# A one-layer hybrid decoder trunk: values times weights by key block, four recurrent heads in one group of score pieces, gates ahead of the attentions, a new order of the first loads

## The chip, the cores and the metric

The kernel runs on one core of one Trainium2 chip. The metric is the device time of one execution in microseconds (us). Of the engines, PE is the matrix engine (PEld its weight loads), DVE the vector engine, ACT the scalar engine, POOL the general one, SP the engine that here only issues DMAs. "PSUM" are the accumulator banks into which PE writes.

## The reference, cut to what matters

```python
# x: 512 tokens x 1024; mem: 256 tokens x 1024; all float32
h = rmsnorm(x, norm_mix)
# one input projection: c_q 384, c_kv 256, k_rope 64, hg q, f, i, g 4 x 512, mem q 512
o_a = mla_group(...)      # 4 heads, 192-wide q and k, causal softmax, values 128 wide
o_b = hgrn2_group(...)    # 4 recurrent heads:
    q = silu(q_raw) * 128 ** -0.5
    f = lb + (1 - lb) * sigmoid(f_raw);  k = 1 - f
    # out_t = sum over s <= t of (q_t . (prod of f over s+1..t) . k_s) v_s
    o = rmsnorm(o, out_gain) * silu(g_raw)
o_c = mem_group(...)      # 4 heads, softmax over the 256 memory tokens
x = x + rmsnorm-ed groups @ w_out
x = x + swiglu(rmsnorm(x), w_gate, w_up, w_down)   # hidden width 2816
```

## The kernel before

**Arithmetic.** Each float32 product of large matrices is done as three matmuls of rounded parts (`mm3`): an operand is split (`split`) into a rounded high part, copied by ACT (`xh`, `wh`, `pth`), and the rest, subtracted by DVE (`xl`, `wl`, `ptl`). Weights come in pieces of 512 columns, so that each piece costs one ACT copy and one DVE subtraction of 128x512.

**Order.** `body` does not issue instructions. A recorder notes each operation with its engine, inputs and a priority (its place in the program, plus a million times its class; `rec.first(0)` is urgent, `rec.first(2)` is filler for gaps). `run` then lists them by a model of prices (`price`), latencies and free buffers (`BUFS`), and everything is issued in that order from line L388, or from line L385 for small matmuls that are packed into column tiles of the array (`tiles`). So L388 and L385 say only which of the two it is; the tile names say what it is. A table `NUDGE` of 17 entries shifts the priority of stretches of operations by hand-chosen numbers.

**Start.** 12 matmuls on a tile of ones run first (`WARM`). ACT's queue issues the five loads of `we`, the weights of the first query and first forget gate (`EARLY`: key, number of 128-row blocks, tag of the buffer), SP's queue the eight blocks of x. Each block is scaled and split, and the 48 matmuls of these two gates follow it. The squares of x give the norm `rx`, and its spread over the partitions is `RX`.

**Recurrent heads.** `hg_in` makes q, k and f of a head (two projections of 24 matmuls, a sigmoid). `hg_levels` works on two heads at a time: for m = 1, 2, 4, 8, 16 it multiplies pieces of 32 tokens (`scores`, a `tiles` group in four column tiles) and DVE puts those of the level into `C` under a mask (`put`); between levels `step_up` multiplies half of q, half of k and the running products `tot`, all on DVE, and the next level's pieces wait for it. m = 32 and m = 64 are single groups of 32- and 64-wide pieces, in two column tiles and in one. `hg_out` multiplies by the values (`pv`), then norms the head (a sum over columns by `colsum`, the root by `rsqrt_col`: ten small DVE operations, `spread`, a scaling). So each pair of heads passes seven groups, and there are 14. Heads 0 and 1 go first, 2 and 3 follow after the value projections (`wide`). The gates of the four heads are in `hg_final`, after the attention on memory is set up.

**Attention.** For the two halves of 256 queries, `softmax` gives rows p, `weights_t` transposes them on PE (`tr<-cst,p`) into the buffers `pth` and `ptl`, and `pv` multiplies them with the values: 2 key blocks for the first half and 4 for the second, each as three matmuls with 256 moving columns. Blocks of p above the diagonal are set to zero and transposed as well. Memory heads do the same with 2 key blocks for either half.

**Rest.** `lowrank` gives the compressed q and kv with a norm of each; `group_norm` norms the three groups, and the output projection and the feed-forward part follow (`fast` for gate and up, `down`).

## Time and profile before

| | us |
|---|---|
| median of 3 runs | 708.37 (707.99 to 708.49) |
| the profiled execution | 707.76 |
| its span in the trace | 706.0 |
| PE busy | 697.1 |
| PEld busy | 581.1 |
| DVE busy | 552.4 |
| ACT busy | 384.8 |
| POOL busy | 93.4 |

The span is the time from the first to the last instruction that the profiler saw; 1.8 us lie around it. A busy PE is not a PE at its peak: a matmul's record has its whole latency, and records overlap, so that the distance between two starts is what one matmul costs. The same holds for DVE: a 128x512 subtraction has a record of 0.69 us, and the next one starts 0.60 us after it. Rows of a timeline merge equal neighbours (x24); rows of the chain of waits give a start, a length, the engine and how many instructions.

### The profile page before, as it was taken

The page shows a single profiled execution, that of the slowest core. Times are in us where ns is not written, and L with a number is a line of the kernel's source. Part 1 is how long each engine was busy: PE and PEld are TensorE (multiplying, and loading weights), DVE is VectorE, ACT ScalarE, POOL GpSimd, SP SyncE. Part 2 cuts the span into 40 slices and gives each one's busy share as a digit, 9 for nine tenths or more (in the row PEclk, how much of TensorE's full clock was granted, in tenths as well). Part 3 has the DMA queues.
Part 4 walks back from the last instruction along what each step waited for, and adds up shares of the span by engine and source line. Part 5 has one row for each costly group of instructions (what it writes and reads, how often), then busy time and mean ns, then how long its engine had stood idle before and what let it go on. Part 6 is the DMA issues. An engine that isn't in the chain of part 4 may idle for free.

```text
span 706.0 us, 13190 instructions
## 1 busy us (share of the span) xinstructions
PE 697.1 (99%) x4813; PEld 581.1 (82%) x4813; DVE 552.4 (78%) x1295; ACT 384.8 (55%) x740; POOL 93.4 (13%) x128
## 2 busy tenths in 40 slices
PE   8999999999999999999999999999999999999997
PEld 5898887787888888888788787888888899999885
DVE  5898879979978899987999969766549767448642
ACT  6653553547765686765767653645553465444320
POOL 0000100000000000000314333032113212310000
PEclk9999999999999999999999999999999999999999
DMA  8232132014511233215999999789868848941241
GB/s 285 78 95 89 64 120 66 32 62 143 185 61 61 75 94 115 77 31 161 266 250 244 221 235 229 203 175 229 190 136 187 165 124 197 218 86 30 72 145 60
DMA packets 47728, 98.05 MB, mean 139 GB/s; under 512 B 5424, under 2 KB 15536, under 8 KB 47664
## 3 DMA queue, kind: packets, MB, share of 16 engines
q1 hardware_dynamic: 33120, 73.10, 32.3%
q0 software_dynamic: 13824, 23.07, 20.5%
q10 hardware_dynamic: 720, 1.05, 0.4%
q8 instruction: 37, 0.61, 0.3%
q14 instruction: 27, 0.22, 0.1%
HBM read 95.11 MB, written 2.10 MB: 138 GB/s over the span
## 4 chain that ended last, share of the span: by engine, by line
PE 91%; DVE 5%; DMA 1%; ACT 1%; issue 1%; SPq 0%; DVEq 0%; ACTq 0%
PE mm L388 46%; PE at L388 21%; PE tr L388 21%; PE at L385 1%; DVE wl L388 1%; DVE y L388 1%; DMA tm<-in_xT 1%; DVE tm L388 1%; DVE td L388 1%; PE tr L385 1%; DMA wr<-in_wf 1%; DVE xl L388 0%; DVE hd L388 0%; DVE v L388 0%; ACT wh L388 0%
## 5 line engine op out<-in xcount | busy, mean ns | idle before, releaser
L388 ACT CAST wh<-wr 128x512 fp32r<-128x512 f32 (+2 forms) x136 | 80.7, 598 | 96.4 <-PE mm L388 49.8
L388 DVE TENSOR_TENSOR wl<-wr,wh 128x512 fp32r<-128x512 f32 (+2 forms) x148 | 96.5, 659 | 31.9 <-issue 12.2
L388 PE MATMUL mm<-xh,wh 128*128 128x512 f32 x248 | 98.1, 398 | 1.4 <-ACT xh L388 1.2
L388 PE MATMUL mm<-xh,wl 128*128 128x512 f32 x248 | 99.0, 399 | 0.4 <-DVE wl L388 0.4
L388 PE MATMUL mm<-xl,wh 128*128 128x512 f32 x248 | 98.7, 399 | 0.3 <-DVE xl L388 0.2
L388 DVE TENSOR_TENSOR wl<-y,wh 128x512 fp32r<-128x512 f32 (+1 forms) x84 | 53.3, 639 | 43.3 <-PE tr L388 17.3
L388 ACT CAST wh<-y 128x512 fp32r<-128x512 f32 (+1 forms) x81 | 46.7, 580 | 67.5 <-PE at L388 36.7
L388 DVE TENSOR_TENSOR wl<-mx,wh 128x512 fp32r<-128x512 f32 (+1 forms) x72 | 45.9, 646 | 28.8 <-PE tr L388 19.3
L388 PE MATMUL mm<-wh,hd 128*128 128x512 f32 (+2 forms) x188 | 63.9, 366 | 0.0
L388 ACT CAST wh<-mx 128x512 fp32r<-128x512 f32 (+1 forms) x67 | 39.2, 586 | 40.9 <-PE at L388 21.6
L388 PEld LDWEIGHTS mm<-xh,wh 128*128 128x128 f32 x248 | 46.5, 188 | 11.1 <-ACT xh L388 2.1
L388 PEld LDWEIGHTS mm<-xl,wh 128*128 128x128 f32 x248 | 46.6, 188 | 10.4 <-DVE xl L388 2.2
L388 PEld LDWEIGHTS mm<-xh,wl 128*128 128x128 f32 x248 | 46.7, 188 | 8.4 <-DVE wl L388 1.0
L388 PE MATMUL at<-wh,hd 128*128 128x512 f32 (+1 forms) x132 | 49.2, 375 | 0.0
L388 POOL DMA_DIRECT2D y<-in_wu x36 | 33.3, 983 | 95.8 <-DVE wl L388 76.3
L388 PE MATMUL tr<-xl,wh 128*128 128x512 f32 x112 | 43.8, 391 | 0.0
L388 PE MATMUL tr<-xh,wh 128*128 128x512 f32 x112 | 43.8, 391 | 0.0
L388 PE MATMUL tr<-xh,wl 128*128 128x512 f32 x112 | 43.7, 390 | 0.0
L388 PEld LDWEIGHTS mm<-wh,hd 128*128 128x128 f32 x188 | 34.5, 188 | 5.0 <-ACT wh L388 0.3
L388 PE MATMUL mm<-wl,hd 128*128 128x512 f32 (+2 forms) x100 | 37.0, 370 | 0.1
L388 PE MATMUL mm<-wh,v 128*128 128x512 f32 (+1 forms) x96 | 36.3, 378 | 0.0
L388 PE MATMUL at<-wh,v 128*128 128x512 f32 (+1 forms) x96 | 35.8, 375 | 0.0
(376 smaller groups left out, 1719.8 us busy)
## 6 DMA issues: line engine op xcount, KB each, us to landing
wr<-in_wf SPq DMA_DIRECT2D x19, 512.0 KB, 3.7
wr<-in_wd SPq DMA_DIRECT2D x16, 512.0 KB, 4.9
mx<-in_wg SPq DMA_DIRECT2D x24, 256.0 KB, 5.2
mx<-in_wu SPq DMA_DIRECT2D x24, 256.0 KB, 5.2
y<-in_wu POOLq DMA_DIRECT2D x24, 256.0 KB, 5.7
tm<-in_xT SPq DMA_DIRECT2D x16, 256.0 KB, 4.2
wr<-in_wt SPq DMA_DIRECT2D x8, 512.0 KB, 4.4
wr<-in_wo SPq DMA_DIRECT2D x8, 512.0 KB, 3.7
```

The costliest lines, as they stand in the source:

```text
L385: r = self.nc.tensor.matmul(get(a), lhsT=get(b), rhs=get(c), start=first, stop=last, skip_group_check=True)
L388: r = getattr(getattr(self.nc, o.eng), o.name)(*[get(a) for a in o.args], **{k: get(a) for k, a in o.kw.items()})
```

## The change

- `pv` goes by key block and makes all 512 queries at once: of the causal case the first key block has 512 moving columns, the second 384, the third and fourth 256, where there were two halves of 256. The third and fourth blocks lie in two new buffers (`pb`). `weights_t` no longer transposes the blocks above the diagonal, and one memset for each part of the weights takes the place of those of p. Memory heads: two key blocks with 512 columns.
- `hg_levels` takes all four heads. A group of scores has 64 pieces of 32x32 for each of m = 1 (with itself), 1, 2, 4, 8 and 16; at m = 32 and 64 heads stand side by side, so that four and two column tiles are used. There are 8 groups where there were 14. DVE's `put` is 128x512.
- The four heads' norms are one sum over columns and one root (`hg_norm`), the two low-rank norms likewise (`rlow`). The gates move to before the attention (`hg_gate`).
- `rsqrt_col` has 8 operations where it had 10, with other constants.
- The rotary part of the queries is transposed for two heads at once, 8 transposes fewer.
- Start: the blocks of x and the pieces of `we` are issued first of all (class -1); ACT's queue has three loads of `we`, SP's the other two between those of x; 10 matmuls on ones.
- The memory's preparation is held behind the norm of x, and its last head's sum of squares is added by a group of its own (`more`). The table `NUDGE` is gone, the price of `tiles` is another one, `hd` has 10 buffers.

```diff
-    NUDGE = ((2868, 2885, -117), (1571, 1576, -1459), ...
-WARM = 12
-EARLY = {0: (1, "p"), 1: (2, "p"), 3: (2, "tc"), 5: (2, "tc"), 7: (1, "tc")}
+WARM = 10
+EARLY = {0: (1, "p"), 1: (1, "p"), 2: (2, "tc"), 4: (2, "tc"), 6: (2, "tc")}
...
-        for k, (n, tag) in EARLY.items():
-            w = ws[k] = sb(tag)[:, :2 * n * P + 8 * (k == 0)]
-            A.dma_start(out=w, in_=t["we"][:, 2 * k * P + 8 * (k > 0):2 * (k + n) * P + 8])
+        xin = []
+        for k in range(KD):
+            if k in EARLY:
+                n, tag = EARLY[k]
+                w = ws[k] = sb(tag)[:, :2 * n * P + 8 * (k == 0)]
+                with rec.first(-1):
+                    (A if k < 4 else DMA).dma_start(out=w, in_=t["we"][:, 2 * k * P + 8 * (k > 0):2 * (k + n) * P + 8])
+            xin.append(sb("tm"))
+            with rec.first(-1):
+                DMA.dma_start(out=xin[k], in_=t["xT"][:, k * S:(k + 1) * S])
...
-    def pv(v, h, pt, ns, y):
-        o = ps_at()[:, 0:256]
+    def pv(v, h, pts, y, causal=False):
+        o = ps_at().rearrange("p (a b) -> p a b", b=P)
         hs = slice(h * P, (h + 1) * P)
-        for s in range(ns):
-            mm3(o, cut(v[s], slice(None), hs), tuple(x[:, 2 * s:2 * s + 2, :].rearrange("p a b -> p (a b)") for x in pt), s == 0, s == ns - 1)
-        A.copy(y, o)
+        ks = [(x, i + 2 * (causal and x is pts[0] and i)) for x in pts for i in range(2)]
+        for s, (x, i) in enumerate(ks):
+            w = tuple(z[:, i::2, :] for z in x)
+            mm3(o[:, NB - w[0].shape[1]:, :], cut(v[s], slice(None), hs), w, s == 0, s == len(ks) - 1)
+        A.copy(y, o.rearrange("p a b -> p (a b)"))
...
+        V.tensor_tensor(C, scores(old), eye.unsqueeze(1).unsqueeze(1).broadcast_to([P, HN, NB, 32]), ALU.mult)
         m = 1
         while m < 128:
+            if m <= 16:
+                put(scores(hs), m)
...
+                w = min(m, 64)
+                o = ps_at()[:, 0:2 * NB * w].rearrange("p (n b t) -> p n b t", t=w, b=NB)
+                at = range(0, P, 2 * m)
+                ks = [(j, b) for j in range(2) for b in range(NB)]
+                T.tiles(o, *[x for h in hs for x in h[:2]], parts=[
+                    (o[i + s * m:i + (s + 1) * m, j, b], hs[2 * s + j][1][:, b * P + i:b * P + i + m], hs[2 * s + j][0][:, b * P + i + m:b * P + i + 2 * m], (j, b) == ks[0], (j, b) == ks[-1])
+                    for j, b in ks for i in at for s in range(2)
+                ])
...
+    def hg_norm(ys):
+        v = small(4 * NB)
+        V.tensor_scalar(v.rearrange("p (h b) -> p h b", b=NB), colsums([sumsq([y], tag=("tc", "td")[h % 2]) for h, y in enumerate(ys)]), RC / P, RC * EPS, ALU.mult, ALU.add)
+        r = rsqrt_col(v, 4 * NB)
+        for h, y in enumerate(ys):
+            V.scalar_tensor_tensor(y, y, smc("g_hg", h), spread(r[:, h * NB:(h + 1) * NB]), ALU.mult, ALU.mult)
...
-    qkf = [hg_in(0), hg_in(1)]
+    qkf = [hg_in(h) for h in range(4)]
...
-    for h, st in enumerate(hg_levels(qkf)):
-        yh.append(hg_out(h, *st))
-    qkf = [hg_in(2), hg_in(3)]
-    for h, st in enumerate(hg_levels(qkf)):
-        yh.append(hg_out(2 + h, *st))
+    qkt = hg_levels(qkf)
...
-    def weights_t(pp_, ns):
-        pt = new_pt(ns)
-        for s in range(0, ns, 2):
-            o = ps_tr()
-            for i in range(4):
-                T.transpose(o[:, i * P:(i + 1) * P], pp_[i % 2][:, (s + i // 2) * P:(s + i // 2 + 1) * P], ident)
+    def weights_t(pp_, s0, q0, pt, causal):
+        o = ps_tr()
+        ends = causal and s0 == q0
+        js = [(q, s) for q in range(2) for s in range(2) if not (ends and s > q)]
+        for i, (q, s) in enumerate(js):
+            T.transpose(o[:, i * P:(i + 1) * P], pp_[q][:, (s0 + s) * P:(s0 + s + 1) * P], ident)
```

ACT's first instructions, before: `p` and `tc` are buffers of `we`, `tm` of x, and a wait on DMAHW is one for a load.

```order
L388 DMA p_1893<-in_we 128x264
L388 DMA p_1906<-in_we 128x512
L388 ACT_TABLE_LOAD
L388 ACTIVATE hpi<-ones 128x1 [waits DVE_49]
L388 DMA tc_1916<-in_we 128x256
L388 DMA tc_1921<-in_we 128x512 [waits DMAHW0_49]
L388 DMA tc_1926<-in_we 128x512 [waits DMAHW2_49]
L388 CAST wh_1937<-p_1893 128x256
L388 ACTIVATE xh_1943<-tm_1897,p_1893 128x512 [waits DMAHW1_49]
```

The same place after the change.

```order
L383 DMA p_1841<-in_we 128x264
L383 DMA p_1850<-in_we 128x256
L383 DMA tc_1856<-in_we 128x512
L383 ACT_TABLE_LOAD
L383 ACTIVATE hpi<-ones 128x1 [waits DVE_49]
L383 CAST wh_1877<-p_1841 128x256 [waits DMAHW0_49]
L383 ACTIVATE xh_1884<-tm_1845,p_1841 128x512 [waits DMAHW1_49]
L383 CAST wh_1890<-p_1850 128x256 [waits DMAHW2_49]
```

The first cast stood behind five loads, two of which waited for others to land; now it stands behind three that wait for nothing.

DVE in the level m = 2 of the first pair of heads, before: `cc` is the score buffer C, `y` and `tm` a head's q and k, and the other `tm` (2256, 2296) its running products.

```order
L388 COPY_PREDICATED cc_2411<-lmask,at_2452 128x256
L388 TENSOR_TENSOR y_2307<-y_2307,tm_2256 128x128x2
L388 TENSOR_TENSOR tm_2268<-tm_2268,tm_2256 128x128x2
L388 TENSOR_TENSOR y_2328<-y_2328,tm_2296 128x128x2
L388 TENSOR_TENSOR wl_2503<-wr_2304,wh_2449 128x512
L388 TENSOR_SCALAR kr<-mm_2254,rx 128x64
L388 TENSOR_TENSOR tm_2256<-tm_2256 128x128
L388 TENSOR_TENSOR tm_2310<-tm_2310,tm_2296 128x128x2
```

DVE in the level m = 1 of the four heads after the change: `tc` is C, and the products lie in `pth` and `ptl`.

```order
L383 COPY_PREDICATED tc_2548<-lmask,at_2551 128x512
L383 TENSOR_TENSOR y_2241<-y_2241,pth_2158 128x256
L383 TENSOR_TENSOR tm_2210<-tm_2210,pth_2158 128x256
L383 TENSOR_TENSOR y_2280<-y_2280,ptl_2214 128x256
L383 TENSOR_TENSOR tm_2247<-tm_2247,ptl_2214 128x256
L383 TENSOR_TENSOR wl_2645<-wr_2336,wh_2624 128x320
L383 TENSOR_TENSOR y_2363<-y_2363,pth_2285 128x256
L383 TENSOR_TENSOR tm_2355<-tm_2355,pth_2285 128x256
L383 TENSOR_TENSOR y_2542<-y_2542,ptl_2387 128x256
L383 TENSOR_TENSOR tm_2461<-tm_2461,ptl_2387 128x256
L383 TENSOR_TENSOR wl_2667<-wr_2403,wh_2642 128x512
```

Between two groups of scores DVE now has a wider put, eight multiplications for four heads, and one or two weight subtractions among them.

PE in the values of the recurrent head 0, second half of the queries, before (`v` are values, `pth` and `ptl` the weights' parts).

```order
L388 MATMUL at_2935<-pth_1901,v_2519 128x256
L388 MATMUL at_2935<-ptl_1904,v_2519 128x256
L388 MATMUL at_2935<-pth_1901,v_2561 128x256
L388 MATMUL at_2935<-pth_1901,v_2526 128x256
L388 MATMUL at_2935<-ptl_1904,v_2526 128x256
L388 MATMUL at_2935<-pth_1901,v_2564 128x256
L388 MATMUL at_2935<-pth_1901,v_2581 128x256
L388 MATMUL at_2935<-ptl_1904,v_2581 128x256
L388 MATMUL at_2935<-pth_1901,v_2592 128x256
```

PE in the values of one recurrent head, all queries, after the change.

```order
L383 MATMUL at_3548<-ptl_3489,v_2778 128x512
L383 MATMUL at_3548<-pth_3474,v_2788 128x512
L383 MATMUL at_3548<-pth_3474,v_2785 128x384
L383 MATMUL at_3548<-ptl_3489,v_2785 128x384
L383 MATMUL at_3548<-pth_3474,v_2796 128x384
L383 MATMUL at_3548<-pb_3526,v_2792 128x256
L383 MATMUL at_3548<-pb_3528,v_2792 128x256
L383 MATMUL at_3548<-pb_3526,v_2804 128x256
L383 MATMUL at_3548<-pb_3526,v_2810 128x256
L383 MATMUL at_3548<-pb_3528,v_2810 128x256
L383 MATMUL at_3548<-pb_3526,v_2826 128x256
```

A head had 18 matmuls of 256 columns in two accumulations (6 and 12) and has 12 in one: three of 512, three of 384, six of 256.

## Rows read from the trace of the kernel before

**Rows 1.** The page: part 1 (busy us, share of the span, instructions of each engine), and part 4 (the chain that ended last, its shares by engine).

```profile
PE 697.1 (99%) x4813; PEld 581.1 (82%) x4813; DVE 552.4 (78%) x1295; ACT 384.8 (55%) x740; POOL 93.4 (13%) x128
...
PE 91%; DVE 5%; DMA 1%; ACT 1%; issue 1%; SPq 0%; DVEq 0%; ACTq 0%
```

**Rows 2.** The table of windows: stretch, its length, busy us of each engine with its instructions, granted PE clock, DMA share, GB/s.

```profile
0.00:20.00 20.00, 17.29 (x60) 12.33 (x61) 12.56 (x24) 13.73 (x25) 1.82 (x9) 1.00 0.72 251
...
40.00:160.00 120.00, 119.12 (x1736) 99.44 (x1725) 102.53 (x327) 56.59 (x121) 2.76 (x11) 1.00 0.22 73
160.00:340.00 180.00, 179.68 (x1134) 148.39 (x1133) 162.94 (x427) 118.11 (x248) 9.74 (x19) 1.00 0.35 106
...
360.00:706.00 346.00, 341.58 (x1647) 288.74 (x1645) 236.38 (x419) 165.77 (x295) 76.81 (x88) 1.00 0.72 168
```

**Rows 3.** Pieces of the chain that ended last: start us, length us, engine and operation, instructions. The four are 128x256 matmuls of `wide`, 128x128 transposes, 128x512 matmuls and 128x384 matmuls of the feed-forward part.

```profile
57.18 0.72 PE mm L388 x6
...
230.50 0.87 PE tr L388 x8
...
461.14 5.44 PE tr L388 x24
...
591.71 0.52 PE mm L388 x3
```

**Rows 4.** Groups of instructions by line and form: the matmuls of weights and values, xcount, then busy us, mean ns of one record.

```profile
L388 PE MATMUL at<-pth,v 128*128 128x256 f32 x96 | 21.2, 291 | 0.0
...
L388 PE MATMUL at<-ptl,v 128*128 128x256 f32 x48 | 14.1, 294 | 0.2 <-DVE ptl L388 0.2
...
L388 PE MATMUL at<-pth,mv 128*128 128x256 f32 x32 | 7.5, 286 | 0.0
...
L388 PE MATMUL at<-ptl,mv 128*128 128x256 f32 x16 | 4.7, 296 | 0.0
```

**Rows 5.** The timeline of PE around four groups of scores (L385): the matmul ahead, the group (the first piece of it at m = 1; a float32 matmul is two records, so 64 matmuls are 128), and the second matmul behind.

```profile
39.37 0.31 PE L388 MATMUL mm<-wh,xh 128*128 128x320 f32 x1
39.61 0.46 PE L385 MATMUL at<-tm,tm 128*32 128x32 f32 x32
...
41.09 0.31 PE L388 MATMUL mm<-wh,xl 128*128 128x320 f32 x1
...
44.46 0.31 PE L388 MATMUL mm<-wl,xh 128*128 128x320 f32 x1
44.70 0.76 PE L385 MATMUL at<-y,tm 128*32 128x32 f32 x64
...
45.64 0.31 PE L388 MATMUL mm<-wh,xh 128*128 128x320 f32 x1
...
62.58 0.28 PE L388 MATMUL mm<-wh,xh 128*128 128x256 f32 x1
62.78 0.70 PE L385 MATMUL at<-y,tm 128*32 128x32 f32 x32
...
63.63 0.28 PE L388 MATMUL mm<-wh,xl 128*128 128x256 f32 x1
...
128.99 0.40 PE L388 MATMUL mm<-xh,wh 128*128 128x512 f32 x1
129.32 1.15 PE L385 MATMUL at<-y,tm 128*64 128x64 f32 x16
...
130.73 0.40 PE L388 MATMUL mm<-xh,wl 128*128 128x512 f32 x1
```

**Rows 6.** The timeline of PE around a sum over columns (16 matmuls, 32 records).

```profile
21.72 0.39 PE L388 MATMUL mm<-xl,wh 128*128 128x512 f32 x1
22.04 0.43 PE L385 MATMUL tr<-ones,td 128*32 128x2 f32 x32
...
22.74 0.40 PE L388 MATMUL mm<-xh,wh 128*128 128x512 f32 x1
```

**Rows 7.** The timeline of all engines in the start: the matmuls on ones, ACT's fourth and fifth load (`ACTq`), its first casts, the first matmul on data; and of PE the first matmul behind the 48 of the first two gates.

```profile
1.22 5.49 PE L388 MATMUL tr<-ones_r 128*128 128x512 f32 x12 [1.22 <-DVE ones_r L388]
...
4.32 2.49 ACTq L388 DMA_DIRECT2D tc<-in_we  x2
6.85 0.40 ACT L388 CAST wh<-p 128x256 fp32r<-128x256 f32 x1 [3.69 <-DMA p<-in_we]
7.16 0.72 ACT L388 ACTIVATE xh<-tm,p 128x512 fp32r<-128x512 f32 x1
...
7.93 0.73 PE L388 MATMUL mm<-xh,wh 128*128 128x512 f32 x2 [1.22 <-ACT xh L388]
...
20.13 0.39 PE L388 MATMUL mm<-xh,wh 128*128 128x512 f32 x1
```

**Rows 8.** The timeline of DVE in the first levels of the second pair of heads.

```profile
106.46 0.45 DVE L388 COPY_PREDICATED cc<-lmask,at 128x256 f32<-128x256 uint8 x1
106.79 0.43 DVE L388 TENSOR_TENSOR tm<-tm,tm 128x256 f32<-128x256 f32 x1
107.12 0.43 DVE L388 TENSOR_TENSOR y<-y,tm 128x256 f32<-128x256 f32 x1
107.46 0.70 DVE L388 TENSOR_TENSOR wl<-wr,wh 128x512 fp32r<-128x512 f32 x1
108.06 0.43 DVE L388 TENSOR_TENSOR tm<-tm 128x256 f32<-128x256 f32 x1
```

More of the change, by code (lines that the diff above doesn't have):

```diff
@@ L189, in price @@
             if o.name == "tiles":
-                return 310 + 1.81 * sum(max(35, self._free(p[2])) for p in o.kw["parts"]) / len({self._rng(p[0])[2] for p in o.kw["parts"]})
+                return 270 + 2.1 * sum(max(35, self._free(p[2])) for p in o.kw["parts"]) / len({self._rng(p[0])[2] for p in o.kw["parts"]})
             if o.name == "transpose":
@@ L542, in colsum, with colsums @@
         return colsums([sq], nblk)[:, 0]
[L544 removed]
+    def colsums(sqs, nblk=NB, more=None):
         o = ps_ts()[:, 0:2 * nblk * len(sqs)]
@@ L548, in colsums @@
         T.tiles(o, ones, *sqs, parts=[
-            (v[g:g + 32, i, b], sqs[i][:, b * P + g:b * P + g + 32], ones, (i, b) == ks[0], (i, b) == ks[-1])
+            (v[g:g + 32, i, b], sqs[i][:, b * P + g:b * P + g + 32], ones, (i, b) == ks[0], (i, b) == ks[-1] and more is None)
             for i, b in ks for g in range(0, P, 32)
         ])
+        if more is not None:
+            T.tiles(o, ones, more, parts=[
+                (v[g:g + 32, 0, b], more[:, b * P + g:b * P + g + 32], ones, False, b == nblk - 1)
+                for b in range(nblk) for g in range(0, P, 32)
+            ])
         return v[..., 0]
@@ L631, in body @@
     early_tr[0] = False
+    normed = rec.last("scalar")
     rec.held = len(rec.ops) - 2
@@ L876, in body @@
     wide(t["wvb"], 256, [ps_mm(), ps_mm(), ps_tr(), ps_tr()], xacts, values_b)
-    for h, st in enumerate(hg_levels(qkf)):
-        yh.append(hg_out(h, *st))
-    qkf = [hg_in(2), hg_in(3)]
-    for h, st in enumerate(hg_levels(qkf)):
-        yh.append(hg_out(2 + h, *st))
+    qkt = hg_levels(qkf)
     mg = []
     ms = None
-    with rec.first(1):
+    with rec.first(1), rec.after(normed):
         for k in range(4):
@@ L1035, in body @@
     V.tensor_tensor(rkn, rk, bc3(rckv, 4), ALU.mult)
+    for h in range(4):
+        hg_gate(h, yh[h])
     def transposed(src, h, scale=None):
```

219 lines of the change are left out of this document (105 added, 114 removed).

## The prediction

> **What bounds the kernel now.** I read the page first: PE has work in 99% of the span and makes 91% of the chain that ended last [rows 1]. The windows say the same of each stage but the first: 17.3 of the first 20 us, 119.1 of 120 us in the recurrent heads, 179.7 of 180 around the attention [rows 2]. So time is won by taking work off PE, and lost only where a new order lets PE wait. What PE's work costs is read from starts, since records overlap: six 128x256 matmuls in 0.72 us (0.120 us each), eight transposes in 0.87 (0.109), 24 matmuls of 128x512 in 5.44 (0.227), three of 128x384 in 0.52 (0.173) [rows 3]. The other engines matter at two places. In the start PE's first matmul on data comes at 7.93 us, when ACT's first copies are there [rows 7]. In the stretch of the recurrent heads DVE is busy for 102.5 of 120 us [rows 2] and stands between one group of scores and the next.
>
> **Part 1: values and transposes.** Before, a causal head has 18 matmuls of 256 columns (2 and 4 key blocks, three each), eight heads 144; the trace has 96 and 48 of them. A memory head has 12, four heads 48; the trace has 32 and 16 [rows 4]. After, a causal head has three of 512, three of 384 and six of 256, a memory head six of 512. Over all: 48 more of 512 (+10.9 us), 24 more of 384 (+4.15), 144 fewer of 256 (-17.3), together **-2.2 us**. The columns above the diagonal that are no longer multiplied would be the gain in streaming alone; the rest is the smaller number of matmuls. Eight transposes of p go (one block of each half, four heads), and eight of the rotary part on balance: 16 x 0.109 = **-1.7 us**. All of this is PE work in stretches where PE never stops [rows 2], so I take it whole; bounds of the two -3 to -4.5.
>
> **Part 2: groups of scores.** The cost of a group is the distance from the matmul ahead of it to the second one behind it, less the two ordinary intervals. With 128 records: 41.09 - 39.37 - 0.29 = 1.43 us; 64 records 45.64 - 44.46 - 0.29 = 0.89; 32 records 63.63 - 62.58 - 0.24 = 0.81; the 64-wide group 130.73 - 128.99 - 0.45 = 1.29 [rows 5]. From the first two, 64 more records cost 0.54 us and a group has a fixed part of 0.35. Before: 2 x 1.43 + 8 x 0.89 + 2 x 0.81 + 2 x 1.29 = 14.2 us. After: six groups with 128 records 8.6, m = 32 with 64 records over four column tiles 0.89, m = 64 with 32 records over two. Before, 16 records of the 64-wide group took 0.94 above the fixed part in one column tile. Side by side the 32 take as long, 1.29; one after the other 2.2. I take 1.29, because 32-wide records plainly ran side by side (64 more in 0.54 us are 8 ns each, and 58 ns each in the 64-wide tile). Sum 10.8, so **-3.4 us**, with -2.5 as the other end.
> No row shows two 64-wide tiles side by side. [...]
>
> **Part 3: sums over columns.** 16 matmuls cost 22.74 - 21.72 - 0.45 = 0.57 us [rows 6]. The four heads' sums become one of 64 matmuls; with the step of the scores (0.27 us for 32 records) that is 0.57 + 3 x 0.27 = 1.4 for 2.3 before (-0.9). The two low-rank sums become one (-0.3). The memory group's sum gets a second group (+0.3 to +0.6). Together **-0.8 us**. The shorter root (two small DVE operations fewer in each) and two table loads fewer on ACT are off PE's path: worth nothing unless PE waits for a norm.
>
> **Part 4: the start.** ACT's first copy of weights is at 6.85 us, behind the fourth and fifth load in ACT's own queue, which stood until another load had landed (4.32 to 6.81); the first block of x is scaled at 7.16, and PE begins at 7.93 [rows 7]. After the change three loads without waits stand there, so ACT can begin when the first weights are there, about 4.3 to 5 us. PE then begins at about 5.7, when ten matmuls on ones are through (twelve took 5.49 us from 1.22: 0.43 each, ten end near 5.5). From there the 48 matmuls need 48 x 0.227 = 10.9 us if fed; before they ended at 20.13, that is in 12.2 us. They will not be fed so early: eight blocks of x still arrive one after the other and DVE makes a subtraction for each block of x and of weights. I expect the end of the 48 near 18.2, **-1.9 us**. Bounds: -0.5 (x comes no sooner, and the two loads of weights now stand in SP's queue between the blocks of x; the norm's sum comes late instead) and -2.7.
>
> **Part 5: new waits.** Four heads in one chain mean that between two groups DVE has a put of 128x512 and eight multiplications of 128x256 at 0.33 us, four small products, and one or two weight subtractions at 0.60 [rows 8]: about 0.6 + 2.7 + 0.7 + 0.6 = 4.6 us, and only up to the last head's multiplication must be waited for, about 4. PE's filler between groups is, by the new order and the intervals above, 0.7, 4.1, 8.9, 4.7, 5.7, 7.0 and 6.6 us. The first pair of groups has no chain between them; the second (27 matmuls of 128x320) is as long as the chain with nothing to spare, and there I expect 0.3 to 0.8 us of wait. What the removed table had gained elsewhere isn't in the trace. Bounds from the rows: PE's idle in the stretch before is 0.9 us of 120 by records [rows 2], so there is at most about 1 us to win; the loss could be 0.5 us at each of eight groups, 4 us. I take **+1.0 us**, near the lower end because PE's list has more filler than before between the later groups. Holding the memory's preparation behind the norm, and the gates ahead of the attention, reorders PE's filler and takes none away; both cost nothing as long as a matmul stands ready, and the cover is the gates' own 96 matmuls (21.8 us at 0.227).
>
> **Sum.** -2.2 - 1.7 - 3.4 - 0.8 - 1.9 + 1.0 = -9.0 us. The profiled execution took 707.76 (706.0 of span and 1.8 around it), the median of the runs is 708.37; the trace is 0.6 below it, and I subtract from the median: **699.4 us**.
>
> **Rivals.** (A) *The four-head chain takes the gain of the groups back.* Each of levels 2, 8 and 16 then waits some 1 us, and `hg_out`, which has its four heads' splits, sums and one common norm in a row, another 2: 5 us, 703.4. For it: one norm for four heads begins only when the last head is there, where single heads could overlap. Against it: the gates and low-rank products are filler there.
> (B) *Slower: DVE bounds the recurrent stretch.* DVE's step-ups, weight subtractions and splits for the fillers stand in one queue. At issue intervals (0.60 and 0.33 us) I count 47 us for DVE between the first group and the last one of the chain, at about the same of PE. If operations that wait for one another pay their whole record (0.69 and 0.43 to 0.45 [rows 8]), 56 us are needed, 9 more, and in the gates that follow some 4: 13 us against a gain of 10, **711**. It decides from the point where DVE's list is longer than PE's by more than 10 us in 16 to 110 us. Against it: in the trace consecutive DVE operations keep the interval also where one reads the other's result a few places on, and the list alternates heads.
> (C) *The start gains nothing.* The x blocks set the pace, not ACT: -0.5 for -1.9, 700.8.
> (D) *The clock stays at half longer.* The matmuls on ones ran at 0.43 us each, twice the later 0.227 [rows 3, 7]. With two fewer and data matmuls that come in ones and twos, PE could be too idle to be granted the full clock. If it is half until 10.5 us, up to 15 matmuls cost 0.2 us more, of which half stands beside waits for x: +1.5, 700.9. [...]
> That the change does not do what it says: only the side-by-side 64-wide tiles could fail in that way (+0.9, 700.3).
>
> **Chances.** The forecast 0.56; C 0.07, D 0.04 and serial 64-wide tiles 0.03, all within 2 us of it; a better order still, more than 2 us below, because the old order's waits go as well, 0.08; A 0.15; B 0.07. The low end of the range has parts 1 to 3 at their best (-4.5 - 3.4 - 1.1 = -9.0), the start at -2.7, waits at -1, and 0.7 for the difference between trace and median: 695.0. The high end is A with 1 us beyond it: 704.5. B and the last of the better orders stay out. A difference of 0.2% (1.4 us) is about what a measurement of this kernel can tell from none: faster by that means below 707.0. All cases but B are; some of A's 0.15 may pile up with a part of B's mechanism and end near the old time, so 0.89 faster, 0.05 the same, 0.06 slower.
>
> **What would show it.** The first data matmul before 6.5 us, and the one behind the 48 near 18.2. Groups with 128 records that cost 1.43 and the 64-wide one 1.3. PE's stop ahead of the second level's group below 1 us, and PE's busy share in the recurrent stretch as before; a DVE that is full there with PE waiting for `y` and `tm` would be B, a gap ahead of the common norm's `spread` would be A. From the attention on, a PE list as dense as before and 4 us shorter. Wrong if PE idles by more than 4 us in all between 20 and 160 us.

## The result and the profile after

| | before | after |
|---|---|---|
| median of 15 runs each (us) | 708.49 | 710.88 |
| lowest and highest | 707.98 to 709.25 | 709.22 to 714.78 |
| ratio, 95% interval | | 1.0044 [1.0034, 1.0055] |
| the profiled execution | 707.76 | 709.22 |
| its span | 706.0 | 707.4 |

The kernel is 2.4 us slower. The prediction said 699.4, in a range of 695.0 to 704.5; the time lies above the range, and on the other side of the kernel before.

The page of the changed kernel, part 1 (busy us, share of the span, instructions), two lines of part 3 (DMA queue, kind: packets, MB, share of 16 engines) and the first line of part 4 (the chain that ended last, by engine); [rows 1] has these of before.

```profile
PE 688.6 (97%) x4755; PEld 574.1 (81%) x4755; DVE 546.7 (77%) x1234; ACT 375.3 (53%) x721; POOL 92.8 (13%) x124
...
q8 instruction: 37, 0.61, 0.3%
...
q14 instruction: 26, 0.21, 0.1%
...
PE 86%; DVE 6%; issue 3%; DMA 3%; ACT 2%; ACTq 0%; POOL 0%; DVEq 0%; POOLq 0%
```

PE is busy for 8.5 us less, as a kernel with less PE work should be, and still ends 1.4 us later: it stands still for about 10 us more. "issue", time in which an engine waited for nothing that the profile shows, is 3% of the chain; it was 1%. The table of windows says where (columns as in [rows 2], with two more stretches; those of before follow it).

```profile
0.00:20.00 20.00, 17.43 (x65) 12.95 (x66) 15.13 (x27) 14.63 (x26) 2.39 (x9) 1.00 0.74 253
20.00:40.00 20.00, 18.55 (x114) 14.80 (x113) 18.35 (x60) 15.20 (x25) 0.00 (x0) 1.00 0.51 159
40.00:160.00 120.00, 113.57 (x1752) 98.06 (x1751) 95.92 (x270) 52.74 (x112) 1.38 (x7) 1.00 0.20 62
160.00:340.00 180.00, 179.05 (x1107) 145.40 (x1107) 163.52 (x430) 113.02 (x241) 9.59 (x20) 1.00 0.34 108
...
420.00:440.00 20.00, 17.45 (x76) 12.91 (x76) 19.08 (x31) 6.78 (x12) 8.03 (x10) 1.00 1.03 232
```

Before:

```profile
20.00:40.00 20.00, 20.00 (x179) 17.15 (x179) 17.97 (x63) 14.82 (x23) 0.00 (x0) 1.00 0.32 95
...
420.00:440.00 20.00, 20.00 (x92) 15.99 (x91) 20.00 (x34) 8.11 (x14) 8.47 (x10) 1.00 1.03 236
```

Three places lost what the rest gained: 40 to 160 us, the recurrent heads (113.57 of 120 us busy, 119.12 before [rows 2]), 20 to 40 us (18.55 of 20, all 20 before), and 420 to 440 us, in the feed-forward part (17.45 of 20, all 20 before). In the recurrent stretch DVE has less to do than before (95.92 for 102.53 us), so it is not DVE's load. What PE waited for in the first 160 us (engine, line, what for: us in total, times, longest):

```profile
PE at L380 <- issue: 4.5, 2, 2.9
PE tr L383 <- DVE ones_r L383: 2.0, 1, 2.0
PE mm L383 <- DVE td L383: 1.5, 1, 1.5
PE at L380 <- DVE tm L383: 1.1, 2, 0.8
```

L380 is the line of small matmuls in column tiles (L385 before), L383 that of all others (L388 before). The largest wait has no releaser at all. The timeline of PE: the start, then three groups of scores, then one with late operands, then the longest stop of the feed-forward part (start us, length us, instruction, count, idle time before it).

```profile
2.00 4.05 PE L383 MATMUL tr<-ones_r 128*128 128x512 f32 x10 [2.00 <-DVE ones_r L383]
5.89 0.62 PE L383 MATMUL mm<-xh,wh 128*128 128x512 f32 x2
...
18.26 0.39 PE L383 MATMUL mm<-xh,wh 128*128 128x512 f32 x1
...
24.35 0.62 PE L383 MATMUL tr<-cst,rx 128*128 128x128 f32 x4
26.66 0.50 PE L383 MATMUL mm<-xh,wh 128*128 128x512 f32 x1 [1.46 <-DVE td L383]
...
58.48 0.46 PE L380 MATMUL at<-pth,tm 128*32 128x32 f32 x32
...
59.33 0.45 PE L380 MATMUL at<-ptl,tm 128*32 128x32 f32 x30
...
60.40 0.31 PE L383 MATMUL tr<-wl,xh 128*128 128x320 f32 x1
60.64 0.86 PE L380 MATMUL at<-y,tm 128*32 128x32 f32 x76
64.39 0.65 PE L380 MATMUL at<-y,tm 128*32 128x32 f32 x52 [2.89 <-issue]
64.98 0.42 PE L383 MATMUL tr<-wh,xl 128*128 128x320 f32 x1
65.23 0.31 PE L383 MATMUL mm<-wh,xh 128*128 128x320 f32 x1
...
80.37 1.13 PE L380 MATMUL at<-y,tm 128*32 128x32 f32 x108
83.09 0.38 PE L380 MATMUL at<-y,tm 128*32 128x32 f32 x20 [1.59 <-issue]
...
104.34 0.50 PE L380 MATMUL at<-y,tm 128*32 128x32 f32 x34
105.62 0.45 PE L380 MATMUL at<-y,tm 128*32 128x32 f32 x30 [0.77 <-DVE tm L383]
...
438.32 0.44 PE L383 MATMUL tr<-cst,ptl 128*128 128x128 f32 x2 [1.74 <-DVE ptl L383]
```

The group at 60.64 (m = 1) and the one at 80.37 (m = 4) stop in their middle. By the measure of [rows 5] the first costs 65.23 - 60.40 - 0.29 = 4.54 us, the second 3.23, where the group at 58.48 costs 1.43. The stop at 61.5 is not a wait for DVE: DVE's product for this group was through at 60.71, before it, and DVE itself then stood still until PE went on. Two lines of DVE's timeline:

```profile
60.02 0.69 DVE L383 TENSOR_TENSOR y<-ptl 128x512 f32<-128x512 f32 x1
...
65.09 0.74 DVE L383 COPY_PREDICATED tc<-lmask,at 128x512 f32<-128x512 uint8 x1 [2.71 <-PE at L380]
```

What does happen at both stops is a transfer on the DMA queue for instructions, q8: from 62.09 to 63.04 us and from 80.86 to 81.80, and PE goes on 1.36 and 1.29 us behind their ends. The page lets one estimate whose instructions: it has 37 transfers of 16 KB (0.61 MB by 37), and PE has 4,755 weight loads and 4,755 matmuls, 9,510; if the transfers are PE's, that is some 257 instructions to each.

### The profile page after: what moved, and what is told of

Read it like the earlier page. It is cut to its first block, busy times and chain, and to the rows that moved or that the text cites. A ratio compares the mean times of both kernels' runs of the same rounds, so it can differ in the third digit from the quotient of the medians.

```text
span 707.4 us, 12975 instructions
## 1 busy us (share of the span) xinstructions
PE 688.6 (97%) x4755; PEld 574.1 (81%) x4755; DVE 546.7 (77%) x1234; ACT 375.3 (53%) x721; POOL 92.8 (13%) x124
## 4 chain that ended last, share of the span: by engine, by line
PE 86%; DVE 6%; issue 3%; DMA 3%; ACT 2%; ACTq 0%; POOL 0%; DVEq 0%; POOLq 0%
PE mm L383 43%; PE tr L383 21%; PE at L383 20%; DMA xl<-in_wg 2%; DVE wl L383 2%; PE at L380 1%; DMA tc<-in_we 1%; DVE hd L383 1%; PE tr L380 1%; ACT wh L383 0%; DVE ptl L383 0%; DVE td L383 0%; DVE qr L383 0%; ACT hd L383 0%; DVE tm L383 0%
## 5 line engine op out<-in xcount | busy, mean ns | idle before, releaser
L383 ACT CAST wh<-wr 128x512 fp32r<-128x512 f32 (+2 forms) x141 | 84.0, 599 | 101.0 <-PE tr L383 44.4
L383 DVE TENSOR_TENSOR wl<-wr,wh 128x512 fp32r<-128x512 f32 (+2 forms) x148 | 96.9, 658 | 33.9 <-issue 11.6
L383 PE MATMUL mm<-xh,wh 128*128 128x512 f32 x248 | 98.0, 398 | 2.0 <-DVE td L383 1.5
L383 PE MATMUL mm<-xh,wl 128*128 128x512 f32 x248 | 98.4, 397 | 0.0
L383 PE MATMUL mm<-xl,wh 128*128 128x512 f32 x248 | 98.1, 396 | 0.1
L383 DVE TENSOR_TENSOR wl<-y,wh 128x512 fp32r<-128x512 f32 (+1 forms) x84 | 53.4, 638 | 41.8 <-PE tr L383 19.3
L383 ACT CAST wh<-y 128x512 fp32r<-128x512 f32 (+1 forms) x82 | 47.4, 581 | 65.9 <-PE at L383 35.5
L383 DVE TENSOR_TENSOR wl<-mx,wh 128x512 fp32r<-128x512 f32 (+1 forms) x72 | 46.1, 645 | 33.5 <-PE tr L383 14.8
L383 PE MATMUL mm<-wh,hd 128*128 128x512 f32 (+2 forms) x176 | 59.7, 366 | 0.7 <-ACT wh L383 0.7
L383 ACT CAST wh<-mx 128x512 fp32r<-128x512 f32 (+1 forms) x67 | 39.0, 585 | 37.2 <-PE at L383 17.7
L383 PEld LDWEIGHTS mm<-xh,wh 128*128 128x128 f32 x248 | 46.6, 188 | 11.5 <-DVE td L383 1.8
L383 PEld LDWEIGHTS mm<-xl,wh 128*128 128x128 f32 x248 | 46.6, 188 | 9.9 <-DVE xl L383 1.0
L383 PEld LDWEIGHTS mm<-xh,wl 128*128 128x128 f32 x248 | 46.7, 188 | 9.0 <-DVE wl L383 0.4
L383 POOL DMA_DIRECT2D y<-in_wu x36 | 32.2, 955 | 104.4 <-DVE wl L383 77.2
L383 PE MATMUL at<-wh,hd 128*128 128x512 f32 (+1 forms) x120 | 45.0, 375 | 0.0
L383 PE MATMUL tr<-xl,wh 128*128 128x512 f32 x112 | 43.8, 391 | 0.0
L383 PE MATMUL tr<-xh,wl 128*128 128x512 f32 x112 | 43.7, 390 | 0.0
L383 PE MATMUL tr<-xh,wh 128*128 128x512 f32 x112 | 43.7, 390 | 0.0
L383 PEld LDWEIGHTS mm<-wh,hd 128*128 128x128 f32 x176 | 32.3, 188 | 5.8 <-ACT wh L383 1.1
L383 PE MATMUL mm<-wh,v 128*128 128x512 f32 (+1 forms) x96 | 35.8, 375 | 0.0
L383 PE MATMUL at<-wh,v 128*128 128x512 f32 (+1 forms) x96 | 35.8, 375 | 0.0
L383 PE MATMUL mm<-wl,hd 128*128 128x512 f32 (+2 forms) x88 | 32.5, 369 | 0.4 <-DVE wl L383 0.4
```

Of the source, the lines that this page charges most:

```text
L383: r = getattr(getattr(self.nc, o.eng), o.name)(*[get(a) for a in o.args], **{k: get(a) for k, a in o.kw.items()})
```

## The experiments

**Theory: PE runs out of instructions.** A group of 64 pieces is 128 weight loads and 128 matmuls, 256 instructions in 1.1 us, by that estimate what one transfer holds. Where such a group uses up a block of 16 KB before the next one is there, PE stands until it lands. Rivals: late operands (DVE), the removed table (`NUDGE`), and the clock.

### Half the instructions, the same groups in the same place

The second and fourth group issue 32 pieces of 64 columns in place of 64 pieces of 32, with the same operands and the same order around them; the products are others. The kernel still waits for everything it waited for, but needs half the instructions there.

```diff
+                if "wider" in o.kw:
+                    seen += 1
+                    if seen in (2, 4):
+                        parts = o.kw["wider"]
...
+            ], wider=[
+                (o[g:g + 32, j, b:b + 2]..., hs[j][1][:, b * P + g:b * P + g + 32], hs[j][0][:, b * P + g:b * P + g + 64], ...)
+                for j, b in ks if b % 2 == 0 for g in range(0, P, 32)
```

> The changed kernel, same order, waits and buffers; only in its second and fourth group of 128 records (m = 1 and m = 4, the two in which PE stops for 2.9 and 1.6 us with no releaser in the profile) a piece has 64 moving columns in place of two pieces of 32, so that these groups have 64 matmuls and weight loads fewer each and write the same columns (what they compute there is not the reference's scores). Theory F (PE runs out of instructions: they come in blocks of 16 KB, and a group of 128 matmuls and 128 weight loads uses up 256 instructions in 1.1 us): both stops go or shrink below 0.5 us each, the profiled time falls from 709.2 by 3 to 5 us, and the granted clock of the runs, which lies between 0.993 and 1.0 for the changed kernel, is 1.0 in nearly all. Theory D (PE waits for DVE's products of the fourth head): the stops stay at 2.5 to 3 and 1.3 to 1.7 us, since the same products are waited for; the time falls by at most 1 us.

Measured: 706.20 us, ratio 0.9965 [0.9952, 0.9978]. The two groups cost 1.22 us each, for 4.54 and 3.23, and PE's waits for "issue" in the first 160 us are 0.7 for 4.5. PE's timeline there:

```profile
61.11 1.10 PE L386 MATMUL at<-y,tm 128*32 128x64 f32 x64
...
64.47 0.30 PE L389 MATMUL tr<-wh,xl 128*128 128x320 f32 x1 [0.31 <-issue]
...
68.47 0.33 PE L386 MATMUL at<-y,tm 128*32 128x32 f32 x16 [0.41 <-issue]
...
78.59 1.10 PE L386 MATMUL at<-y,tm 128*32 128x64 f32 x64
```

The stops hang on the number of instructions, not on operands: those were the same. What is left of the first one no longer lies in its group but among ordinary matmuls, behind as many PE instructions as before (478 weight loads in either kernel). At a granted clock of 1.0 the runs took 704.01 and 705.30 us, for 709.22 to 709.52 of the changed kernel, about what the theory had (3 to 5 us less); the profiled run, 706.74, had lost some of its clock. The second expectation, that the clock would then stay open in nearly all runs, failed. The granted clock of its runs is 0.997 to 1.0, and the windows of the profiled one (columns as above) show where it falls: behind the stop in the feed-forward part, which is still there.

```profile
432.00:436.00 4.00, 2.04 (x10) 0.98 (x8) 4.00 (x8) 0.17 (x1) 0.86 (x1) 0.89 1.10 263
436.00:440.00 4.00, 4.00 (x18) 3.25 (x18) 3.30 (x6) 2.40 (x5) 2.62 (x3) 0.68 0.70 94
440.00:444.00 4.00, 4.00 (x25) 3.39 (x24) 3.99 (x7) 3.17 (x7) 0.86 (x1) 1.00 1.02 201
```

Behind this stop (1.7 us) PE is granted 0.89 and 0.68 of the clock. The lower clock is taken as a half: the trace of the changed kernel has 0.50 behind its last instruction (708.4 to 709.0 us). By that it lasted for an estimated (1 - 0.89) x 4 / 0.5 = 0.9 us in the first stretch and (1 - 0.68) x 4 / 0.5 = 2.6 in the second, 3.4 us in all, which cost an estimated 1.7.

### Groups of two heads again

```diff
-            o = ps_at().rearrange("p (n b t) -> p n b t", t=32, b=NB)
+            o = ps_at()[:, 0:HN * NB * 32].rearrange("p (n b t) -> p n b t", t=32, b=NB)
...
-    qkt = hg_levels(qkf)
+    qkt = hg_levels(qkf[:2]) + hg_levels(qkf[2:])
```

> The changed kernel with the score groups by two heads as before (14 groups with at most 64 records, all else of the change kept). Theory F: no stop without a releaser between 40 and 130 us; the groups cost some 4 us more than eight groups without stops would (14.4 to 15 us in all where the changed kernel has 17.5), so the time falls by 2 to 3 us below 709.2 and the granted clock is 1.0. Theory D or a chain that is too long: much the same. If neither holds and the rest of the change is what costs, 709 to 711 us.

Measured: 708.70 us, 1.0009 [1.0, 1.0018]. No wait for "issue" in the recurrent stretch; the 16 groups (two of them run side by side) cost 15.2 us in all, for 17.5 of the eight. So the fewer groups, which should have saved 3.4 us, cost 2 us against the many.

### The four-head group as two halves

The group of 64 pieces is listed as two of 32, one behind the other, which other work may part.

```diff
-            T.tiles(o, *[x for h in hs for x in h[:2]], parts=[
...
+            for js in (range(0, HN // 2), range(HN // 2, HN)):
+                T.tiles(o, *[x for j in js for x in hs[j][:2]], parts=[
```

> The changed kernel with each four-head group of scores (m = 1 with itself to 16) recorded as two groups of two heads into the same bank, with one put as before; the list then sets ordinary matmuls between the halves. Same matmuls, same products, six more fixed parts of 0.35 us (+2.1). Theory F (instructions run out in a group of 128 matmuls and 128 weight loads): stops without a releaser shrink from 4.5 us to below 1; net 2 to 3 us less than the changed kernel, 707.5 to 709. If they were only waits for the fourth head, 4.5 us of waits would stay in sum, and the time rises to 712 or more.

Measured: 711.85 us, 1.0047 [1.0035, 1.0059]. The waits for "issue" fall to 1.0 us, but the time, expected at 707.5 to 709, does not fall: there are six more fixed parts, and the order that follows has a new wait of 1.4 us for DVE's `v` (those for `ptl` and `tm`, 3.9 us, were 3.4 before). The mechanism is borne out, the remedy is worthless.

### The other way round: twice the pieces in the kernel before

If supply is the cause, the kernel before must stop too when its two groups of 128 records, which cost 1.42 us [rows 5], issue every piece twice (values of these groups doubled).

```diff
+                parts = o.kw["parts"]
+                if len(parts) == 64:
+                    parts = parts[:-1] + [p[:4] + (False,) for p in parts[-1:]] + [p[:3] + (False, p[4]) for p in parts]
```

> The kernel before, in its own order, with the pieces of its two m = 1 groups issued twice into the same bank (128 matmuls in place of 64; the scores there are doubled, not the reference's). Nothing else is made to wait. Theory F: a block of 256 instructions then lies wholly within the group and is used up in 1.1 us, where the stopped blocks of the changed kernel took 5.2 from end to end; so each of the two groups costs 1.1 us more for its matmuls and a stop of 2 to 4 us on top, and the time rises by 5 to 10 us to 713 to 718, with a granted clock below 1.0 in some runs. Without F: 2.2 us more in all, 710 to 711, and no stop without a releaser.

Measured: 717.75 us, 1.0129 [1.0114, 1.0145]. The groups cost 5.08 and 5.19 us, of which 4.9 are two stops without a releaser:

```profile
41.08 0.41 PE L388 MATMUL at<-tm,tm 128*32 128x32 f32 x27
43.86 0.22 PE L388 MATMUL at<-tm,tm 128*32 128x32 f32 x2 [2.37 <-issue]
...
109.84 0.21 PE L388 MATMUL at<-tm,tm 128*32 128x32 f32 x2
112.56 0.46 PE L388 MATMUL at<-y,tm 128*32 128x32 f32 x31 [2.50 <-issue]
```

Of the 9.3 us, 2.2 are the doubled matmuls (128 records at 1.1 us, twice) and 5.2 the stops (3.66 + 3.76 more for the two groups, less 2.2); stretches at half the clock (granted clock 0.994 to 0.997 in the runs) can account for the rest, some 2 us. The profiled run has one behind the second stop, from 113.9 us (128x512 matmuls start 0.43 us apart from 114.07 to 117.06, 0.23 apart ahead of it and behind it), and one in the start, at 8.0 (0.96 granted in 0 to 39 us).

### Groups held apart

The groups of m = 2, 4 and 8 are held until a given matmul of the fillers is through, so that other blocks fall on them; one shift of the table is in it as well (below).

```diff
+HOLD = {2: 28, 4: 56, 8: 63}
...
+            with rec.after(marks[HOLD[m]] if m in HOLD else None):
```

> The changed kernel with the table entry put back and three groups of scores (m = 2, 4, 8) held in the planner until a later matmul of the value projections, so that the same groups of 128 matmuls lie elsewhere among the ordinary matmuls; same work, same groups. In the changed kernel both stops without a releaser began at weight loads number 478 and 860, 3 x 128 less 2 apart, so theory F puts the ends of PE's blocks of 256 instructions at 94 + 128 j. Counted over the new order with the traced intervals, the blocks that end at loads 478, 606, 734 and 862 take 6.6 us or more, and only the one that ends at load 1118 (within the group of m = 8) is short, 3.0 us. F: no stop in the groups of m = 1, 2 and 4, and one of 1 to 2.2 us near load 1118 in the group of m = 8; 0.5 to 3 us less than with the entry alone (708.9). If the stops hang on the group (its data, its level) and not on the place in the instruction stream, those of m = 1 and m = 4 remain.

Measured: 709.40 us, 1.0015 [1.0006, 1.0024]. The group of m = 4 no longer stops; m = 1, which follows the first group after 2 us as before, does, at the same place.

```profile
60.93 0.86 PE L385 MATMUL at<-y,tm 128*32 128x32 f32 x76
64.62 0.65 PE L385 MATMUL at<-y,tm 128*32 128x32 f32 x52 [2.83 <-issue]
...
85.31 1.30 PE L385 MATMUL at<-y,tm 128*32 128x32 f32 x128
...
92.91 1.30 PE L385 MATMUL at<-y,tm 128*32 128x32 f32 x128
...
115.76 1.28 PE L385 MATMUL at<-y,tm 128*64 128x64 f32 x32
```

The stop that was expected in the group of m = 8 did not come; it had been worked out for an order with the group of m = 1 standing later, which is not what ran. So a stop can be moved by moving a group, but this run alone does not give a rule for where one falls. The last row settles another question: the 64-wide pieces of two heads cost 1.41 us in two column tiles (by the same measure), not the 2.2 of one behind the other.

The traces of all versions, read together, do give a rule. Count PE's instructions from its first one: weight loads, matmuls and its few others. All 18 stops for "issue", in ten traces, begin when 256 k + 193 of them are through: 961 and 1,729 in the changed kernel (k = 3 and 6), 961 and 1,217 with wider pieces, 961 with groups held, 705 and 2,753 with the pieces doubled. Each ends 1.2 to 1.6 us behind the end of the k-th transfer on q8. At the 508 block ends of all fourteen traces PE never goes on sooner than 1.2 us behind the end of that transfer, and the transfer itself starts at most 298 instructions ahead. So what PE lacks is its next block of 256 instructions, and where the k-th transfer ends in time there is no stop.

### The table

The kernel before with an empty table:

```diff
-    NUDGE = ((2868, 2885, -117), (1571, 1576, -1459), ...
+    NUDGE = ()
```

> The kernel before without its NUDGE table, nothing else. If the removed table is what the changed kernel lacks in the feed-forward part (PE idle 3.8 us between 420 and 440 us, where DVE's subtractions stand behind its sums), this kernel has a stop of 2 to 4 us at about the same place and takes 711 to 714 us. If the stop comes from the rest of the change, it stays at 708 to 709.5 us.

Measured: 712.17 us, 1.0056 [1.0043, 1.0069]: the table was worth some 4 us. But its stop is another than that of the changed kernel, before 337.80 us, not at 436:

```profile
337.80 0.96 PE L388 MATMUL mm<-xh,wh 128*128 128x512 f32 x3 [2.25 <-ACT xh L388]
```

Then the changed kernel with one entry: the first 60 operations on the gate weights of the feed-forward part (22 loads, 12 copies and subtractions, 26 matmuls) stand 113 places earlier. The old table had the same shift for the same operations, as (3804, 3864, -113).

```diff
+    NUDGE = ((3623, 3683, -113),)
...
+        for a, b, d in self.NUDGE:
+            for o in ops[a:b]:
+                o.prio += d
```

> The changed kernel with one entry of the old table put back at the same operations (loads and products of the second pass over the gate weights, priority -113). If the order there is what makes PE stop between 420 and 440 us, that idle falls from 3.8 to below 1 us and the time by 2.5 to 4 us. If DVE has too much work there in any order, nothing moves (within 1 us).

Measured: 708.86 us, 1.0008 [0.9998, 1.0018]. In 420 to 440 us PE is busy for 18.97 us (17.45 without the entry), so the idle time there falls to 1.0 us and not below, and the waits for "issue" stay (4.0). With the two halves above the same entry gives 709.28 for 711.85:

> The last one, with the one table entry of the gate weights' second pass put back too. If the two losses are separate, both go: 2 us below the last one, 705.5 to 707, and the first version that is faster than the kernel before with the reference's output. If they are not, the same as the last one.

Measured: 1.0013 [1.0005, 1.0022], short of the 705.5 to 707 that was expected: the halves had their own losses (above). With groups of two heads it gives 707.08 for 708.70 (diffs as above, `NUDGE = ((3637, 3697, -113),)`):

> The changed kernel with score groups of two heads (no group with more than 64 records but one) and the one table entry of the gate weights' second pass. If the two losses are what stands between the changed kernel and its forecast, both are gone: 2 us below the version with pairs alone (708.7), 706 to 707.2, faster than the kernel before by 0.15 to 0.3%, with PE's idle between 420 and 440 us at 2.4 or less. If the list scheduler's order moves the loss elsewhere, 708 to 709.

Measured: 0.9976 [0.9966, 0.9986], a clock of 0.999 to 1.0 in all runs, and faster than before. So one entry is worth 2.0, 2.6 and 1.6 us by the medians, and 2.3 to 2.6 by the ratios, each of which is taken against the kernel before of its own session.

### The start

The changed kernel with the start of before (12 matmuls on ones, five loads of `we` in ACT's queue, x loaded block by block):

```diff
-WARM = 10
-EARLY = {0: (1, "p"), 1: (1, "p"), 2: (2, "tc"), 4: (2, "tc"), 6: (2, "tc")}
+WARM = 12
+EARLY = {0: (1, "p"), 1: (2, "p"), 3: (2, "tc"), 5: (2, "tc"), 7: (1, "tc")}
...
-            r = xin[k]
+            r = sb("tm")
+            DMA.dma_start(out=r, in_=t["xT"][:, k * S:(k + 1) * S])
```

> The changed kernel with the start of before: 12 matmuls on ones, five loads of the early weights on ACT's queue, loads of x between the splits as before. If the new start gains the 1.9 us that were forecast, this one is 1.5 to 2 us slower than the changed kernel's 709.2 at full clock, and its PE reaches the spread of the norm (RX) at 25.7 us where the changed kernel does at 24.4. If what was gained is given back in the wait of 1.5 us behind that spread (26.7 us), both reach the 140th matmul at the same time and the time is within 0.7 us.

Measured: 710.34 us, 1.0033 [1.002, 1.0046], 0.5 below the change whole, with intervals that overlap. The first spread of the norm stands at 24.66 us there and at 24.35 with the new start, and what follows waits for DVE's `td` until 26.69 and 26.66. So no gain of the new start is left there.

The copy of ones before PE's first matmul takes DVE 1.00 us, for 0.21 before, while POOL clears two `tm` buffers (0.88 to 1.87 us). To tell whether that is the cause, these clearings were put behind the norm:

```diff
+            with rec.after(normed):
+                G.memset(A_, 0.0)
```

> The changed kernel with POOL's memsets of the four score tiles (128x512) held until the norm of x, so that they don't run beside DVE's first copy (ones, 1.00 us in the changed kernel and 0.21 before). If they are what slows that copy, PE's first instruction is at 1.2 us, where the changed kernel has it at 2.0, the clock opens 0.8 us sooner, and the time falls by 0 to 0.8 us (the first matmul on data then waits for ACT). If not, the copy stays at 1.0 us.

Measured: 710.73 us, 1.0031 [1.0018, 1.0043]. They moved in the list only: POOL had nothing ahead of them and ran them at 0.88 us as before, and the copy still took 1.00. So this run does not answer the question. Nor does any run show that an earlier first instruction of PE opens the clock sooner: the kernel before has the first at 1.22 us and the full clock from 7.1, the changed kernel 2.00 and 5.2.

### A version that is faster than both

Groups of two heads, one entry, and the projections of the third and fourth head behind the value projections, as before the change; the new values, sums, gates and start stay.

```diff
-    qkf = [hg_in(h) for h in range(4)]
+    qkf = [hg_in(0), hg_in(1)]
...
+    qkf += [hg_in(2), hg_in(3)]
     qkt = hg_levels(qkf[:2]) + hg_levels(qkf[2:])
```

> The version with pairs and the entry (707.08), with the order of stages of before as well: two heads' projections, then the value projections, then the other two heads. In the changed kernel all four heads' projections come first; PE's next matmul behind the norm's spread then needs a PSUM bank that DVE empties only after the norm (wait of 1.5 us at 26.7 us). If that is where the gain of the start goes, the wait is below 0.4 us, and the time falls by 1 to 1.5 us, to 705.5 to 706.1. If the norm itself is late, PE waits there on other matmuls and the time stays within 0.5 us.

Measured: 705.79 us, 0.9961 [0.9948, 0.9973], faster than before and than the change. The windows, columns as above:

```profile
20.00:40.00 20.00, 20.00 (x258) 17.14 (x257) 18.28 (x65) 15.77 (x28) 0.00 (x0) 1.00 0.48 148
40.00:160.00 120.00, 118.64 (x1621) 99.52 (x1620) 99.22 (x279) 55.00 (x113) 1.41 (x7) 1.00 0.21 70
...
420.00:440.00 20.00, 18.96 (x83) 14.15 (x82) 20.00 (x34) 7.68 (x13) 8.44 (x10) 1.00 0.94 204
```

PE no longer waits at 26 us, and is nearly as dense in the recurrent stretch as before (119.12 [rows 2]); 1 us of standing is left in 420 to 440 us. One stop for "issue" is left too, 0.69 us at 151 us, in a sum over columns.

## Why the prediction was wrong

Where the 1.4 us between the two spans come from. PE's work is the count of records of each form by the intervals of [rows 3]; "stood" is what a stretch has beyond that and beyond its groups and sums, which are measured as in [rows 5].

| | predicted | measured | how |
|---|---|---|---|
| 1 values, transposes | -3.9 | -4.0 | PE's work without groups and sums 656.7 to 652.3, less 0.45 for two fewer matmuls on ones |
| 2 groups of scores | -3.4 | +2.7 | 14.8 (14 groups) to 17.5 (8 groups) |
| 3 sums over columns | -0.8 | -1.2 | 10.2 to 9.0 |
| 4 start | -1.9 | -0.1 | those 0.45; first instruction of PE at 2.00 for 1.22 (+0.8); stood -1.9 behind it to 20 us, +1.5 in 20 to 40 |
| 5 new waits | +1.0 | +4.1 | stood +3.8 in 420 to 440 us, +1.6 in 160 to 420, -1.0 behind 440, -0.3 in 40 to 160 |
| sum | -9.0 | +1.5 | the spans differ by +1.4 |

The waits for `tm` in two groups are in line 2. The medians differ by 2.4, 1.0 more than the spans: the changed kernel was granted 0.993 to 1.0 of the clock in its runs (709.22 to 709.52 us at 1.0, 713.26 to 714.78 at 0.993), and the profiled run was one at 1.0.

**Part 1** was right, in mechanism and size; the columns above the diagonal were PE time. The -4.0 is counted, not timed by itself: the records of each form number what was forecast, and a matmul of each form has the same interval in both traces.

**Part 2 is the step that failed.** Its prices were right for a group that runs through: without the two stops (3.1 and 1.8 us more than 1.43) and without the waits for `tm` (1.0 and 0.8), the eight groups cost 17.5 - 4.9 - 1.8 = 10.8 us, the sum that the prediction had, and the 64-wide tiles stand side by side (1.41 us). What the step took for granted is that six groups of 128 records cost what one of them does in [rows 5]. There two such groups were 64 us apart; now two stand 2 us apart (58.48 and 60.64) and the rest 8 to 11 us, and of these one more stopped (80.37). PE's supply of instructions was not among the costs, and no rival had it. That the stops are this and not DVE is shown by the run with half the instructions (0.7 us left of 4.5) and the one with twice as many in the kernel before (there, 2.4 and 2.5 us). That a block of 256 instructions is what runs out, is shown by where all 18 stops begin and by the transfers behind which they end.

**Part 3** was right, with 0.4 us more.

**Part 4** had the mechanism and not the worth. The first matmul on data stands at 5.89 us (forecast 5.7; 7.93 before [rows 7]), and the 49th one near 18.3 (18.2; 20.13). The 5.89 is in part luck: ten slow matmuls on ones from 2.00 us would have ended near 6.3, but from the ninth on they ran at full rate (starts 0.43 us apart up to 5.16, 0.23 from 5.43 on). The clock's record in the trace has the full clock from 5.2 us, that of before from 7.1 (4.5 to 8.2 in all traces); the windows count the time ahead of it as 1.00. And PE's first instruction comes 0.8 us later, since the copy of ones takes longer, the first spread is only 1.4 us earlier than before (24.35 for 25.74), and the wait behind it, 1.46 us for DVE's `td`, takes that back: with all four heads' projections ahead, nothing else stood ready for PE there. This was the cover that the part didn't name. Rival C (the start gains little) was right in kind, for another reason than x being late; undone by itself, the start makes no difference clear of noise (0.5 us the other way). The last experiment, with other work in that place, has no such wait.

**Part 5** looked at DVE between groups and bounded it by 0.5 us a group: two such waits came, 1.8 us by what the groups cost. It set down what the removed table gains elsewhere as not in the trace, and took nothing for it: 3.8 us were lost in one place of the feed-forward part, where PE stood for `ptl` and `wl` of DVE, and one entry of the table gives back some 2.4. That the rest of the 3.8 is the table's too is not shown. Since its stop is not the one that the kernel before shows without its table, no run of that kernel would have told its place.

**The sign and the rivals.** The prediction was to be wrong if PE idles by more than 4 us between 20 and 160 us; it idles there for 1.5 + 6.4 = 7.9. A did not come: the common norm shows no gap, and the groups of m = 2, 8 and 16 did not wait as it said. B did not come, DVE's load fell. D did not come: the full clock came at 5.2 us in the start, for 7.1 before, and no trace shows D's 10.5; but the clock did cost time elsewhere (0.993 granted in the slowest runs). Slower was given 0.06, by B alone: the right sign for the wrong reason.

**What stays open.** Which blocks come late. The stops fell only at ends of blocks of 256 instructions, but 18 of 508 ends have one, and the k-th transfer starts anywhere from 298 to 0 instructions ahead of the end where it is needed; what sets its start was not found. Whether the 1.00 us of the copy of ones comes from the clearing of `tm` beside it stays open too: the run meant for it did not part the two.

The best version is 6.4 us above the forecast of 699.4: some 4.4 for the groups of scores (16 of them cost 15.8 us, 1.0 more than the 14 of before, where 3.4 less was forecast); 0.8 for the copy of ones; some 2 (by starts) for the feed-forward part; the rest, some 0.8 in its favour, was not followed.

## What to carry to other kernels

Count instructions as well as their time: joining groups of small matmuls saves fixed parts (an estimated 0.35 us each, from [rows 5]), but 256 PE instructions in 1.1 us can make PE wait for instructions (here 3 us where two such groups stood 2 us apart), and wider pieces, half the instructions for the same operands, took most of that away. A stop without a releaser is looked for in the instruction queue: count PE's instructions up to it. An order tuned by hand belongs to its kernel: when such a table goes, run the kernel before without it for the size, and look for stops far from the edit for the place. A gain at the head of a chain is worth what stands ready behind it; name that work before the gain is counted.

## What the runs showed of the hardware that was not expected

- PE stood up to 2.9 us in the middle of a group of small matmuls, all operands there. All 18 stops without a releaser begin 193 instructions behind a multiple of 256 and end 1.2 to 1.6 us behind the end of a 16 KB transfer on the queue for instructions, which starts at most 298 instructions ahead. Wider pieces cut the stops (4.5 to 0.7 us), more pieces made them (0 to 4.9).
- PE's clock was halved for an estimated 3.4 us at a time, an estimated 1.7 us lost in each, away from the start: behind PE's stop at 433 us in the run with wider pieces, and behind 2.25 us of waiting at 337.8 us without the table (PEclk 0.57 in 339 to 343 us, (1 - 0.57) x 4 / 0.5 = 3.4; 128x512 matmuls start 0.43 us apart from 339.60 to 340.88 and 0.23 from 342.85 on). With groups held it was halved behind 155 us (PEclk 0.96 in 152 to 156 us, 0.62 in 156 to 160), where there was no long stop, but three short waits (1.0 us) and two sums with two columns a matmul, PE busy for 3.37 of 4 us. It comes in some executions and not in others: the changed kernel was granted 0.993 to 1.0 in its runs, and its stop before 438 us, with PE busy for 1.9 of 4 us, closed nothing in the profiled run (PEclk 1.00 in 436 to 444 us). What halves the clock, and what sets the length, no run shows.
